# A rotary embedding on one core: the first reads all on one queue, x's first piece in three row groups ahead of the tables

## The chip, the cores and the metric

The kernel runs on one core of a Trainium2 chip. Its time is the device time of an execution in microseconds (us), and the figure for a kernel is the median of its runs. One more execution was recorded by the hardware profiler; all busy times, waits and transfers below are of that one.

## The reference

x has 8 images of 2048 positions, 8 heads and 64 numbers a head, all float32; the two tables, cos and sin, have 32 numbers for each position. The head's two halves are rotated against each other:

```python
x1 = x[..., : x.shape[-1] // 2]
x2 = x[..., x.shape[-1] // 2 :]
cos = cos[None, :, None, :]
sin = sin[None, :, None, :]
out1 = x1 * cos - x2 * sin
out2 = x1 * sin + x2 * cos
return np.concatenate([out1, out2], axis=-1)
```

Each image is 4.19 MB. All of x is read once and all of the output written once, 33.55 MB each way, and each table adds 0.26 MB.

## The kernel before

**Tiling.** The 2048 positions of an image are laid on 128 partitions, 16 positions to a partition, so that a partition ("row" below) holds 16 x 512 numbers, 32 KB, which lie in one run in memory. An image has one tile `xt` (five buffers, so that images 5 to 7 reuse those of 0 to 2), is computed in place, and is stored from the same tile. A unit (`UNIT`, L30) is a quarter of a row: 2048 numbers, 8 KB.

**Reads.** At the head of the program, the sines are read on the scalar queue (L74, into `sin_sb`), the cosines on the sync queue (L75, into `cos_sb`), and then `load` (L64 to L68) is called for images 0 to 4 on the sync queue. Image 0 is read in three pieces, of one, one and two units a row (1, 1 and 2 MB), all 128 rows each; the other images in one transfer of 4 MB. Images 5 to 7 are loaded as soon as image b - 5's arithmetic is written down in the program; the load itself waits until that image's stores have landed.

**Tables.** The scalar engine makes `nsin`, the sines with the other sign, and a copy of the sines in PSUM, `sin_ps` (L89, L90). The vector engine copies the cosines to PSUM, `cos_ps` (L92). GpSimd builds a unit matrix `eye` (L79, L80).

**Arithmetic.** `rotate` (L101) takes one piece of an image. In the usual kind, "A", GpSimd makes the sine products, one multiply for each half of the heads (L121, with `sin_sb` and then `nsin`); the vector engine makes the cosine products (L128) and adds the two into `xt` (L135). In kind "B", for the first unit of images 2, 4 and 5, the addition is done by the matrix engine with the unit matrix (L142, L143) and copied back by the scalar engine (L144). In kind "C", for the first unit of images 1 and 3, the vector engine makes the sine products too (L147), and the matrix engine adds (L159, L160, L164). Image 0 is computed in pieces of half a unit twice and then whole units, image 7 in whole units and at its end two halves.

**Stores.** `store` (L70 to L72) writes image 0 in three shares and images 1 to 6 in one, on the scalar queue; image 7 goes out in three shares (2, 1 and 1 MB) on the sync queue. A store is issued when the last addition of its share is done.

**Order.** `keep` holds the marked instructions of an engine in the order in which the program lists them. Each queue's transfers are issued in that order. The framework gives each transfer one of eight semaphores in turn, over both queues; a transfer that takes one over waits, before it is issued, for the transfer that had it before.

Of the kernel before, what the change touches and what calls it, by code (L numbers as in the profile page):

```python
# [10 lines left out]
def kernel(  # L11
# [7 lines left out]
    nc = tc.nc  # L19
    keep = tc.keep_in_program_order  # L20
# [5 lines left out]
    P = 128  # L26
# [8 lines left out]
    xv = x.rearrange("b (q r) h d -> b q (r h d)", q=P)  # L35
    ov = out.rearrange("b (q r) h d -> b q (r h d)", q=P)
    cos_src = cos.rearrange("(q r) d -> q r d", q=P)
    sin_src = sin.rearrange("(q r) d -> q r d", q=P)
# [9 lines left out]
    cos_sb = const_pool.tile([P, R, Dh], f32, tag="cb")  # L48
    sin_sb = const_pool.tile([P, R, Dh], f32, tag="sb")
# [8 lines left out]
    def spans(sizes):  # L58
        lo = 0
        for n in sizes:  # L60
            yield lo, n
            lo += n

    def load(b):  # L64
        xt = xpool.tile([P, ROW], f32, tag="xt", name=f"xt{b}")
        for lo, n in spans([UNIT, UNIT, 2 * UNIT] if b == 0 else [ROW]):
            keep(nc.sync.dma_start(out=xt[:, lo : lo + n], in_=xv[b, :, lo : lo + n]))  # L67
        xts[b] = xt  # L68

    def store(b, lo, n):  # L70
        queue = nc.sync if b == last else nc.scalar
        keep(queue.dma_start(out=ov[b, :, lo : lo + n], in_=xts[b][:, lo : lo + n]))  # L72

    keep(nc.scalar.dma_start(out=sin_sb, in_=sin_src))  # L74
    keep(nc.sync.dma_start(out=cos_sb, in_=cos_src))  # L75
    for b in range(NBUF):
        load(b)

# [2 lines left out]
        out=eye,  # L81
        in_=eye,
# [100 lines left out]
    for b in range(B):  # L183
        done = 0
        outs = list(spans(shares(b)))
        for lo, n in spans(pieces(b)):
            rotate(b, lo, n)
            done = lo + n
            while outs and sum(outs[0]) <= done:
                store(b, *outs.pop(0))  # L190
        if b + NBUF <= last:
            load(b + NBUF)
# [30 lines left out]
```

## Time and profile before

| | |
|---|---|
| median of 3 runs | 163.28 us (163.25 to 163.31) |
| the profiled execution, its own time | 163.36 us |
| its span, first to last instruction | 161.5 us |
| VectorE busy | 140.1 us (87%) |
| GpSimd busy | 138.9 us (86%) |
| TensorE matmuls busy | 49.8 us (31%) |
| ScalarE busy | 12.8 us (8%) |
| moved by DMA | 67.65 MB |
| GpSimd idle ahead of its first multiply, waiting for x | 6.0 us |

The span is shorter than the time of the execution by 1.86 us that lie around it. Busy times are of the five engines that compute; the transfers are done by 16 DMA engines beside them, which a queue of SyncE (q1 in the profile) and one of ScalarE (q10) feed. The page cuts the span into 40 slices of 4.04 us. "To landing" is the time from the issue of a transfer until its data is there, so it includes what the transfer stands in the queue. The chain of waits goes back from the last instruction: each step is what released the step after it.

At the head, the profile shows this in order of time: both tables are issued at 0.73 us, the cosines landing 3.7 and the sines 4.0 us later; x's first piece is issued at 1.15 us and lands after 6.0 us. VectorE's copy of the cosines runs at 4.46 us, its first multiply at 7.27, GpSimd's first multiply at 7.31, and the first addition at 9.81.

### The profile page before, as it was taken

What the parts mean: (1) busy time and instruction counts of PE and PEld (TensorE: products, weight loads), DVE (VectorE), ACT (ScalarE), POOL (GpSimd) and SP (SyncE); (2) the same over time, 40 slices, a digit from 0 to 9 for tenths busy, and PEclk for the clock granted to TensorE, in tenths of its full rate; (3) what the DMA queues carried; (4) which work ended last, traced back from release to release, by engine and by line L of the source; (5) the groups of instructions that cost most, each with busy time, mean ns of one, the idle gap of its engine ahead of it and who ended that gap; (6) DMA issues with size and microseconds to landing.
All of it is one profiled execution on the core that took longest, in us unless ns stands there. A gap on an engine that the chain in (4) does not pass through costs nothing.

```text
span 161.5 us, 460 instructions
## 1 busy us (share of the span) xinstructions
PE 49.8 (31%) x80; PEld 18.7 (12%) x80; DVE 140.1 (87%) x66; ACT 12.8 (8%) x14; POOL 138.9 (86%) x70
## 2 busy tenths in 40 slices
PE   0000000397507790788019741975000000000000
PEld 0000000132103230223014211421000000000000
DVE  0369899999999999999999999999899998999900
ACT  3300000002200201011200220022000000000000
POOL 1199999999999899999995999998999979999200
PEclk9999999999985899569955996599855555555555
DMA  4999999999999999999999998999999999999894
GB/s 147 432 448 418 438 438 454 406 406 503 389 389 446 422 495 389 422 487 389 422 487 389 438 473 381 438 471 398 446 448 406 438 454 406 438 454 434 377 422 211
DMA packets 3458, 67.65 MB, mean 419 GB/s; under 512 B 384, under 2 KB 384, under 8 KB 768
## 3 DMA queue, kind: packets, MB, share of 16 engines
q1 hardware_dynamic: 2016, 38.01, 55.3%
q10 hardware_dynamic: 1440, 29.62, 42.6%
q14 instruction: 2, 0.02, 0.0%
HBM read 34.08 MB, written 33.55 MB: 419 GB/s over the span
## 4 chain that ended last, share of the span: by engine, by line
DMA 46%; DVE 37%; POOL 9%; issue 2%; SPq 0%; DVEq 0%; POOLq 0%; ACTq 0%
DMA xt<-in_x_dram 28%; DVE t L128 18%; DMA out_dram<-xt 18%; DVE xt L135 17%; POOL t L121 9%; DVE t L147 1%; SPq L75 0%; DVEq L135 0%; POOLq L121 0%; SPq L67 0%; ACTq L72 0%
## 5 line engine op out<-in xcount | busy, mean ns | idle before, releaser
L121 POOL TENSOR_TENSOR t<-xt,sin_sb 128x1024 f32<-128x1024 f32 (+1 forms) x32 | 70.3, 2196 | 10.9 <-DMA xt<-in_x_dram 8.2
L128 DVE TENSOR_TENSOR t<-xt,cos_ps 128x2048 f32<-128x2048 f32 (+1 forms) x34 | 73.4, 2166 | 2.9 <-DMA xt<-in_x_dram 2.1
L121 POOL TENSOR_TENSOR t<-xt,nsin 128x1024 f32<-128x1024 f32 (+1 forms) x32 | 70.2, 2195 | 0.0
L135 DVE TENSOR_TENSOR xt<-t,t 128x2048 f32<-128x2048 f32 (+1 forms) x29 | 62.2, 2145 | 5.9 <-POOL t L121 3.4
L142 PE MATMUL o<-t,eye 128*128 128x512 f32 x24 | 17.3, 811 | 22.8 <-DVE t L128 19.3
L159 PE MATMUL o<-t,eye 128*128 128x512 f32 x16 | 12.1, 850 | 38.5 <-DVE t L128 36.3
L143 PE MATMUL o<-t,eye 128*128 128x512 f32 x24 | 14.9, 709 | 0.0
L144 ACT COPY xt<-o 128x1024 f32<-128x1024 f32 x6 | 6.1, 1012 | 45.7 <-PE o L143 45.7
L142 PEld LDWEIGHTS o<-t,eye 128*128 128x128 f32 x24 | 5.6, 256 | 32.2 <-issue 26.3
L159 PEld LDWEIGHTS o<-t,eye 128*128 128x128 f32 x16 | 3.7, 256 | 44.0 <-POOL t L121 30.9
L164 ACT COPY xt<-o 128x1024 f32<-128x1024 f32 x4 | 4.0, 1012 | 50.4 <-PE o L160 39.4
L143 PEld LDWEIGHTS o<-t,eye 128*128 128x128 f32 x24 | 5.7, 239 | 8.3 <-issue 8.3
L160 PE MATMUL o<-t,neye 128*128 128x512 f32 x8 | 6.4, 887 | 0.2 <-DVE t L147 0.2
L92 DVE COPY cos_ps<-cos_sb 128x512 f32<-128x512 f32 x1 | 0.7, 695 | 4.5 <-DMA cos_sb<-in_cos_dram 4.5
L147 DVE TENSOR_TENSOR t<-xt,sin_ps 128x2048 f32<-128x2048 f32 x2 | 4.6, 2280 | 0.0
L160 PE MATMUL o<-t,eye 128*128 128x512 f32 x8 | 4.1, 592 | 0.0
L160 PEld LDWEIGHTS o<-t,neye 128*128 128x128 f32 x8 | 2.2, 305 | 5.3 <-issue 3.7
L160 PEld LDWEIGHTS o<-t,eye 128*128 128x128 f32 x8 | 1.5, 190 | 1.9 <-issue 1.9
L89 ACT ACT_TABLE_LOAD x1 | 1.3, 1283 | 1.2 <-PEq L207 1.2
L89 ACT ACTIVATE nsin<-sin_sb 128x512 f32<-128x512 f32 x1 | 0.6, 630 | 2.3 <-DMA sin_sb<-in_sin_dram 2.3
L90 ACT COPY sin_ps<-sin_sb 128x512 f32<-128x512 f32 x1 | 0.6, 578 | 0.0
L79 POOL MEMSET eye<- 128x128 f32 x1 | 0.2, 204 | 0.3 <-POOLq L207 0.3
(6 smaller groups left out, 1.0 us busy)
## 6 DMA issues: line engine op xcount, KB each, us to landing
xt<-in_x_dram SPq DMA_DIRECT2D x7, 4096.0 KB, 39.1
out_dram<-xt ACTq DMA_DIRECT2D x6, 4096.0 KB, 28.0
xt<-in_x_dram SPq DMA_DIRECT2D x2, 1024.0 KB, 7.0
xt<-in_x_dram SPq DMA_DIRECT2D x1, 2048.0 KB, 12.5
out_dram<-xt ACTq DMA_DIRECT2D x1, 2048.0 KB, 25.1
out_dram<-xt SPq DMA_DIRECT2D x1, 2048.0 KB, 12.4
out_dram<-xt SPq DMA_DIRECT2D x2, 1024.0 KB, 8.7
out_dram<-xt ACTq DMA_DIRECT2D x1, 1536.0 KB, 19.9
```

Source lines behind the costliest of these rows:

```text
L89: keep(nc.scalar.mul(nsin, sin_sb, -1.0))
L92: keep(nc.vector.tensor_copy(cos_ps, cos_sb))
L121: nc.gpsimd.tensor_mul(out=t2u[:, :, u, :].rearrange("p (r h) d -> p r h d", h=H), in0=xu[:, :, 1 - u, :].rearrange("p (r h) d -> p r h d" ...
L128: nc.vector.tensor_mul(out=t1.rearrange("p (r k d) -> p r k d", r=nr, d=Dh), in0=xk, in1=rep(cos_ps[:, r0 : r0 + nr, :], 2 * H),)
L135: keep(nc.vector.tensor_add(out=xt, in0=t1, in1=t2))
L142: nc.tensor.matmul(oc, eye, t1[:, cs], start=True, stop=False)
L143: nc.tensor.matmul(oc, eye, t2[:, cs], start=False, stop=True)
L144: keep(nc.scalar.copy(xt[:, 2 * j * C : 2 * (j + 1) * C], o))
L147: nc.vector.tensor_mul(out=t2.rearrange("p (r k d) -> p r k d", r=nr, d=Dh), in0=xk, in1=rep(sin_ps[:, r0 : r0 + nr, :], 2 * H),)
L159: nc.tensor.matmul(oc, eye, t1u[:, gs, u, :], start=True, stop=False)
L160: nc.tensor.matmul(oc, eye if u else neye, t2u[:, gs, 1 - u, :], start=False, stop=True)
L164: nc.scalar.copy(xu[:, :, u, :], o.rearrange("p (g d) -> p g d", d=Dh))
```

## The change

All reads at the head are issued on the sync queue. `load` splits the first piece of image 0 (one unit a row) into three transfers by rows: rows 32 to 95, then 0 to 31, then 96 to 127. Right after them, from inside `load`, the sines and the cosines are read, and then image 0's other two pieces and the images 1 to 4 as before. The scalar queue reads nothing any more and only stores. The arithmetic, the pieces it is cut into, and the stores are the same. The lines of the file below `load` move down by up to nine and, behind the two removed lines, by seven.

```diff
     def load(b):
         xt = xpool.tile([P, ROW], f32, tag="xt", name=f"xt{b}")
         for lo, n in spans([UNIT, UNIT, 2 * UNIT] if b == 0 else [ROW]):
-            keep(nc.sync.dma_start(out=xt[:, lo : lo + n], in_=xv[b, :, lo : lo + n]))
+            first = b == 0 and lo == 0
+            for p, q in ((32, 96), (0, 32), (96, P)) if first else ((0, P),):
+                keep(
+                    nc.sync.dma_start(
+                        out=xt[p:q, lo : lo + n], in_=xv[b, p:q, lo : lo + n]
+                    )
+                )
+            if first:
+                keep(nc.sync.dma_start(out=sin_sb, in_=sin_src))
+                keep(nc.sync.dma_start(out=cos_sb, in_=cos_src))
         xts[b] = xt
 
     def store(b, lo, n):
         queue = nc.sync if b == last else nc.scalar
         keep(queue.dma_start(out=ov[b, :, lo : lo + n], in_=xts[b][:, lo : lo + n]))
 
-    keep(nc.scalar.dma_start(out=sin_sb, in_=sin_src))
-    keep(nc.sync.dma_start(out=cos_sb, in_=cos_src))
     for b in range(NBUF):
         load(b)
```

## The prediction

> **What bounds the kernel now.** I read the page's DMA rows first, then the busy times slice by slice, then the chain of waits, then the two ends of the span in time.
>
> ```profile
> GB/s 147 432 448 418 438 438 454 406 406 503 389 389 446 422 495 389 422 487 389 422 487 389 438 473 381 438 471 398 446 448 406 438 454 406 438 454 434 377 422 211
> DMA packets 3458, 67.65 MB, mean 419 GB/s; under 512 B 384, under 2 KB 384, under 8 KB 768
> q1 hardware_dynamic: 2016, 38.01, 55.3%
> q10 hardware_dynamic: 1440, 29.62, 42.6%
> ```
>
> The two queues hold the 16 DMA engines busy for 97.9% of 161.5 us. Per engine q1 (SyncE's, mostly reads) moves 38.01 MB / (0.553 x 16 x 161.5 us) = 26.6 GB/s, and q10 (ScalarE's, mostly writes) 29.62 / (0.426 x 16 x 161.5) = 26.9 GB/s: the same fixed rate per engine in both directions, some 430 GB/s together.
>
> The same in windows (last columns: share of the DMA engines' time, then GB/s):
>
> ```profile
> 1.00:1.50 0.50, 0.00 (x0) 0.00 (x0) 0.00 (x0) 0.33 (x1) 0.29 (x1) 1.00 0.00 0
> 1.50:2.00 0.50, 0.00 (x0) 0.00 (x0) 0.00 (x0) 0.50 (x1) 0.00 (x0) 1.00 0.67 66
> 2.00:2.50 0.50, 0.00 (x0) 0.00 (x0) 0.00 (x0) 0.45 (x1) 0.00 (x0) 1.00 0.18 20
> 2.50:3.00 0.50, 0.00 (x0) 0.00 (x0) 0.00 (x0) 0.00 (x0) 0.00 (x0) 1.00 0.83 213
> 3.00:3.50 0.50, 0.00 (x0) 0.00 (x0) 0.00 (x0) 0.00 (x0) 0.00 (x0) 1.00 0.99 385
> 3.50:4.00 0.50, 0.00 (x0) 0.00 (x0) 0.00 (x0) 0.00 (x0) 0.00 (x0) 1.00 1.23 479
> 4.00:40.00 36.00, 7.86 (x11) 2.92 (x12) 30.57 (x17) 2.36 (x4) 32.69 (x17) 1.00 1.02 434
> 40.00:130.00 90.00, 41.96 (x71) 15.80 (x69) 87.40 (x39) 9.11 (x9) 86.19 (x38) 0.77 1.00 432
> 130.00:159.00 29.00, 0.00 (x0) 0.00 (x0) 22.14 (x12) 0.00 (x0) 19.35 (x11) 0.50 0.99 427
> ```
>
> From 4 to 159 us the transfers never pause: 434, 432 and 427 GB/s. So the end is the start of the transfers plus 67.65 MB at that rate. Only the first 4 us are poor: they move (66 + 20 + 213 + 385 + 479) x 0.5 us = 0.58 MB, which at 432 GB/s is 1.35 us of work, so 2.65 us are lost before the stream is at speed.
>
> GpSimd and VectorE are nearly as full (86% and 87%), and the chain of waits runs through them, so I check whether they set the end instead:
>
> ```profile
> 63.33 29.16 DMA out_dram<-xt
> 92.56 39.12 DMA xt<-in_x_dram
> 131.81 4.61 POOL t L121 x2
> ```
>
> ```profile
> out_dram<-xt SPq DMA_DIRECT2D x1, 1024.0 KB, 7.3
> ```
>
> The second fence is the last store, issued at 153.40 (143.50 + 10.24 less its own 0.34 us). It moves 1.05 MB, 2.4 us at 432 GB/s, and with some 1.5 us for start and landing (the tables' first packets come about 1 us after their issue at 0.73) it would need 3.9 us; it takes 7.3. It stands about 3.4 us in a queue that is still full. The store of 29.16 us and the load of 39.12 us are likewise 4.19 MB each (9.7 us alone): queueing, not work. So an earlier or later computation changes nothing until it is more than about 3 us late at the end.
>
> **The change, part by part.** Bytes and packet sizes stay: the pieces of x keep 8 KB a row, the tables 2 KB a row. The two table reads move behind x's first piece and one of them changes queue; the first piece becomes three transfers.
>
> *(a) What the start-up slices hold.* In 1.5 to 2.5 us the engines moved 43 KB, 21 packets of 2 KB (the tables'), a little over one for each of the 16 engines; the packet records begin at 1.77 us. In that time packets came one by one, not at the rate of their bytes. Now 8 KB rows stand there. If the same 21 packets move, it is 172 KB instead of 43, and 129 KB at 432 GB/s are 0.30 us; an 8 KB packet, 8192 B / 26.6 GB/s = 0.31 us, fits between them. The slice 2.5 to 3.0 (213 GB/s) should fill up partly as well; half of its shortfall, 0.25 us, brings 0.12. I take 0.4 us of gain. Bounds: nothing, if the delay is of time and of bytes alike; 0.9 us, if the stream runs at full rate from 1.77 us on (4.00 - 1.77 - 1.35). A loss here I exclude: nothing is put ahead of the first transfer on SyncE, which still goes out at 0.73.
>
> *(b) Issuing.* SyncE issues seven transfers where it issued four, one each 0.47 us (starts 1.15, 1.63, 2.10). x's 64 rows are 0.52 MB, 1.2 us of transfer, the 32-row pieces 0.26 MB, 0.6 us each at full rate, the tables 0.6 us each: the list of work grows faster than it empties. Cost 0, hidden by the transfers ahead. If that cover were gone it would be two issues, 0.94 us, which I do not add to the range. In the compiled order x's image 1 now waits, before its issue, for the 64-row piece to land (images 2 to 4 for the sines, the cosines and x's last piece of image 0; before, images 2 to 4 waited for the sines and two x pieces). That is near 4 us, and x's two further pieces, 3.15 MB or 7.3 us, are queued by then; only SyncE's later loads stand behind it. Cost 0. ScalarE's queue loses one issue of 0.40 us ahead of a table load it has to do anyway; nobody waits for that.
>
> *(c) The 32-row pieces.* The trace has no transfer of fewer than 128 rows, so the price is bounded. At the rate of all rows, each 0.26 MB takes 0.61 us and the split is free: 0. That every engine keeps 26.6 to 26.9 GB/s on reads and writes alike says that a fixed path limits it, not the memory. If that path belongs to the engine, 32 rows go at full speed; if it belongs to the rows, 16 engines now crowd into a quarter of them. At half rate each piece takes 1.22 us, and both lose 2 x 0.61 = 1.22 us. The 64 rows could lose as much again, 1.22 us, if they too are too few; I take 0, because they move while the start-up leaves the engines waiting for time and not for bytes, and leave the upper end to the last tenth of the range. For the two pieces, between 0 and 1.22 the rows do not decide. I take 1.0 us: half rate, less some 0.2 us in which engines that share rows are out of step (the packet records show the engines ending the cosines up to 0.5 us apart, most within 0.2). The pieces stand one behind the other in each engine's list, which is why I let the second not run beside the first.
>
> [...]
>
> *(d) The computation's start.* GpSimd's first multiply (7.31 us) needs the whole first piece and the sines; VectorE's (7.27) the piece and the cosines. The bytes ahead of both are the same 1.57 MB. With (a) and (c) all three have landed at about 7.2 + 0.6 = 7.8 us; the sines 0.6 us before, near 7.2, so GpSimd starts about as before. The cosines come last: copy 0.69 us, then VectorE's multiply at 8.5 instead of 7.27. But the addition behind it waits for GpSimd's second multiply (9.81 now), so 8.5 + 1.23 = 9.7 still fits. Cost 0, covered by the 3.4 us at the end; without that cover up to 0.6 us.
>
> Sum: -0.4 + 0 + 1.0 + 0 = +0.6 us on the profiled execution's span of 161.5, so 162.1; with the 1.86 us that lie outside the span (163.36 - 161.5) 163.96, and less 0.08, by which that execution was above the median of 163.28, **163.9 us**. A measurement of this kernel tells about 0.2%, 0.33 us, from no change.
>
> **The rivals.** *Full rate for the 32 rows.* The path belongs to the engine, (c) costs nothing, (a) stays: 163.28 - 0.4 = 162.9, down to 162.4 with all of 0.9. For it: constant 26.6 and 26.9 GB/s per engine. Against: all rows of the trace give each engine its own eight rows, so they can't tell. It decides for faster when the two pieces together lose under 0.1 us. *Gain and loss cancel*, engines out of step by enough that (c) is 0.2 to 0.6, or the change of order does nothing and the pieces little: 163.3, within 0.3. For it: the spread of 0.5 us between engines. *The computation sets the end after all*: then GpSimd's start counts. At full rate the piece and the sines land one table (0.6 us) and the start-up gain (0.4) earlier, so the time is 163.28 - 1.0 = 162.3. Against: the last store's 3.4 us of queue. *Stores crowd out the last load*: an earlier first store takes turns with the loads sooner, image 7 lands later and its 21.6 us of arithmetic (131.81 to 153.38) end later; it decides from 3.4 us, the queue's slack, and a shift of 1 to 2 us in the load leaves it unused: 163.3, or 164.5 if the shift were 4.6 us.
>
> **How the numbers follow.** Forecast 58%, own range 163.5 to 164.5, the upper end being (c) whole and (a) nothing, 163.28 + 1.22 = 164.5; about 51 points of it lie above 163.61 and 7 within 0.2%. Full rate 27%: 18 points faster, 9 within. Cancelling 10%, all within. The computation 4%, faster. Stores 1%, slower. Together faster 0.22, same 0.26, slower 0.52. The range 162.7 to 164.5 leaves out the lower part of the full rate's bounds, the computation's case and a slow 64-row piece.
>
> **What would show it.** Right: the 8 KB packets of the first piece move more in 1.5 to 2.5 us than 43 KB; then a dip to about 215 GB/s for some 2 us between 3 and 6 us; from there 430 GB/s to the end, and the last store still queueing about 7 us. Each 32-row piece should land about 1.2 us after the one ahead. Wrong: landings 0.6 us apart and no dip (full rate), a start-up like before, (a) failing, or a pause in the transfers after 100 us, which would mean that the computation decides.

## The result, and the profile after

The changed kernel takes 164.71 us (median of 4 runs, 164.60 to 164.78), against 163.28 before on the same chip: slower by 1.43 us, a ratio of 1.0087 with a 95% interval of 1.0070 to 1.0105. The profiled execution took 164.78 us with a span of 163.0.

The windows of the changed kernel at the head (columns as above: the last two are the share of the DMA engines' time and GB/s):

```profile
1.50:2.00 0.50, 0.00 (x0) 0.00 (x0) 0.00 (x0) 0.50 (x1) 0.00 (x0) 1.00 0.00 0
2.00:2.50 0.50, 0.00 (x0) 0.00 (x0) 0.00 (x0) 0.01 (x1) 0.00 (x0) 1.00 0.85 147
2.50:3.00 0.50, 0.00 (x0) 0.00 (x0) 0.00 (x0) 0.00 (x0) 0.00 (x0) 1.00 0.82 197
3.00:4.00 1.00, 0.00 (x0) 0.00 (x0) 0.00 (x0) 0.00 (x0) 0.00 (x0) 1.00 0.84 336
4.00:5.00 1.00, 0.00 (x0) 0.00 (x0) 0.00 (x0) 0.00 (x0) 0.00 (x0) 1.00 1.17 320
5.00:6.00 1.00, 0.00 (x0) 0.00 (x0) 0.00 (x0) 0.00 (x0) 0.00 (x0) 1.00 0.91 217
6.00:7.00 1.00, 0.00 (x0) 0.00 (x0) 0.00 (x0) 0.00 (x0) 0.00 (x0) 1.00 0.95 219
7.00:8.00 1.00, 0.00 (x0) 0.00 (x0) 0.00 (x0) 0.00 (x0) 0.00 (x0) 1.00 1.09 399
```

From 5 to 7 us the engines are busy 91% and 95% of the time, and move 217 and 219 GB/s, half of the 430: they are not waiting, their packets take longer. From 5 to 6 us these are mostly the rows of x's 32-row pieces, from 6 to 7 us mostly those of the tables, which are queued behind them and have all 128 rows. And the first slice that moves anything is 2.0 to 2.5, where before it was 1.5 to 2.0. The records of the single packets say the same (8 KB packets are x's rows, 2 KB packets the tables'):

```
                              before      after
first packet of the stream    1.77 us     2.11 us
8 KB packet, median           309 ns      309 ns from 3.0 to 4.0 us, 519 to 577 ns from 4.5 to 6.0 us
2 KB packet, median           84 ns       139 to 152 ns from 5.5 to 7.0 us, then 85 to 89 ns
```

The loss can be added up in two windows, before and then after:

```profile
0.00:4.00 4.00, 0.00 (x0) 0.00 (x0) 0.00 (x0) 1.28 (x1) 0.70 (x6) 1.00 0.49 145
4.00:10.00 6.00, 0.00 (x0) 0.00 (x0) 2.12 (x3) 1.35 (x3) 2.69 (x3) 1.00 1.03 438
```

```profile
0.00:4.00 4.00, 0.00 (x0) 0.00 (x0) 0.00 (x0) 1.28 (x1) 0.70 (x6) 1.00 0.42 127
4.00:10.00 6.00, 0.00 (x0) 0.00 (x0) 0.56 (x1) 1.22 (x3) 1.07 (x1) 1.00 1.03 335
```

In the first 4 us the changed kernel moves (145 - 127) x 4 us = 0.07 MB less, 0.17 us at 432 GB/s; in the next 6 us (438 - 335) x 6 us = 0.62 MB less, 1.43 us. Together 1.6 us, and the span grew by 1.5. (A window counts a packet whole where it starts; with packets that cross an edge shared out, the second figure is 1.3 us.)

The chain of waits of the changed kernel tells another story. Its shares by line:

```profile
by line: DVE t L135 35.3%; DVE xt L142 29.9%; POOL t L128 17.1%; issue 5.8%; DMA sin_sb<-in_sin_dram 3.9%; DVE t L154 1.3%; SPq L70 1.0%; DVEq L142 0.3%; POOLq L128 0.0%
```

The long transfers that stood in it before are gone; it is now arithmetic from the sines to the end, and GpSimd's first multiply begins at 8.93 us instead of 7.31, 1.62 us later, about what the kernel lost. So two readings give the same number, and the time alone can't choose between them: the stream of transfers lost 1.5 us, or the computation began 1.6 us late.

### The profile page after: what moved, and what is told of

Read it like the earlier page. It is cut to its first block, busy times and chain, and to the rows that moved or that the text cites. A ratio compares the mean times of both kernels' runs of the same rounds, so it can differ in the third digit from the quotient of the medians.

```text
span 163.0 us, 464 instructions
## 1 busy us (share of the span) xinstructions
PE 49.0 (30%) x80; PEld 18.4 (11%) x80; DVE 140.1 (86%) x66; ACT 12.8 (8%) x14; POOL 139.1 (85%) x70
## 4 chain that ended last, share of the span: by engine, by line
DVE 66%; POOL 17%; issue 6%; DMA 4%; SPq 1%; DVEq 0%; POOLq 0%
DVE t L135 35%; DVE xt L142 30%; POOL t L128 17%; DMA sin_sb<-in_sin_dram 4%; DVE t L154 1%; SPq L70 1%; DVEq L142 0%; POOLq L128 0%
## 5 line engine op out<-in xcount | busy, mean ns | idle before, releaser
L166 PE MATMUL o<-t,eye 128*128 128x512 f32 x16 | 12.0, 842 | 40.2 <-POOL t L128 32.5
L149 PE MATMUL o<-t,eye 128*128 128x512 f32 x24 | 16.7, 787 | 23.5 <-DVE t L135 20.1
L150 PE MATMUL o<-t,eye 128*128 128x512 f32 x24 | 14.9, 709 | 0.0
L167 PE MATMUL o<-t,eye 128*128 128x512 f32 x8 | 4.1, 592 | 0.0
```

Of the source, the lines that this page charges most:

```text
L149: nc.tensor.matmul(oc, eye, t1[:, cs], start=True, stop=False)
L150: nc.tensor.matmul(oc, eye, t2[:, cs], start=False, stop=True)
L166: nc.tensor.matmul(oc, eye, t1u[:, gs, u, :], start=True, stop=False)
L167: nc.tensor.matmul(oc, eye if u else neye, t2u[:, gs, 1 - u, :], start=False, stop=True)
```

## The experiments

All figures are medians with the ratio to the kernel before on the same chip. "Stream" below is the two-window sum above, worked out for each kernel from its one profiled execution: the bytes by which it falls short of the kernel before from 0 to 4 and from 4 to 10 us, divided by 432 GB/s.

**Which of the two sets the end.** The kernel before, with GpSimd made late by work that nothing needs:

```diff
+    waste = const_pool.tile([P, 4, Dh], f32, tag="waste")
+    for _ in range(12):
+        keep(nc.gpsimd.tensor_mul(out=waste, in0=nsin[:, :4, :], in1=sin_sb[:, :4, :]))
```

> The kernel before with twelve multiplies of 128x128 on GpSimd that nothing needs, ahead of its first multiply, so that it begins some 1 to 2 us later; all transfers as before. Theory (transfers set the end): 163.3 us, the last store queues that much less than 7.3 us. Rival (the computation sets it): the time grows by what GpSimd's first multiply is later than 7.31, to 164.3 to 165.3 us.

163.48 us, ratio 1.0014 (1.0005 to 1.0022). GpSimd came even later than meant; its timeline in this run:

```profile
10.87 0.45 POOL L96 TENSOR_TENSOR waste<-nsin,sin_sb 128x128 f32<-128x128 f32 x1
11.28 1.25 POOL L125 TENSOR_TENSOR t<-xt,sin_sb 128x512 f32<-128x512 f32 x1
```

The first multiply began 3.97 us later, and the time grew by 0.16. The last store shows where the rest went:

```profile
out_dram<-xt SPq DMA_DIRECT2D x1, 1024.0 KB, 4.0
```

It was issued 3.44 us later than before, at 156.84 us, and lands 4.0 us after its issue, where before it took 7.3: the 3.3 us are the queue that it no longer stood in, and 4.0 is close to the 3.9 us that such a store was reckoned to need by itself. The computation has some 3.4 us to spare at the end. In the changed kernel the last store, issued at 154.92 us, still takes 7.1, so it is not the computation that lost the time, whatever the chain of waits runs through.

**Split or order.** The changed order with the first piece in one transfer (against the kernel before, with the lines between left out):

```diff
             keep(nc.sync.dma_start(out=xt[:, lo : lo + n], in_=xv[b, :, lo : lo + n]))
+            if b == 0 and lo == 0:
+                keep(nc.sync.dma_start(out=sin_sb, in_=sin_src))
+                keep(nc.sync.dma_start(out=cos_sb, in_=cos_src))
 ...
-    keep(nc.scalar.dma_start(out=sin_sb, in_=sin_src))
-    keep(nc.sync.dma_start(out=cos_sb, in_=cos_src))
```

> The changed order without the split: x's first piece as one transfer of all 128 rows, then sines and cosines, all on the sync queue. Theory (the stream of transfers sets the end; the 32-row pieces move at half rate, some 1.3 us, and the start-up got some 0.2 us worse): 163.5 us, packets of 8 KB at 309 ns throughout. Rival (the computation sets the end, and it began 1.6 us later in the changed kernel, at 8.93 instead of 7.31): here GpSimd should begin near 6.8 to 7.0, so 162.8 to 163.0 us. If the order and not the split is what cost, 164.7 us.

163.46 us, ratio 1.0008 (1.0000 to 1.0017). GpSimd's first multiply began at 6.20 us, 1.1 us earlier than before, and no time was gained by it. And the split with the tables first, on two queues as before:

```diff
-            keep(nc.sync.dma_start(out=xt[:, lo : lo + n], in_=xv[b, :, lo : lo + n]))
+            for p, q in ((32, 96), (0, 32), (96, P)) if b == 0 and lo == 0 else ((0, P),):
+                keep(nc.sync.dma_start(out=xt[p:q, lo : lo + n], in_=xv[b, p:q, lo : lo + n]))
```

> The split without the changed order: both tables first on their two queues as before, then 64, 32 and 32 rows. Theory: 163.28 + 1.3 = 164.6 us, a dip to about 200 to 250 GB/s of some 2.4 us, and a start-up like before. If the split is free and the order cost: 163.3 us. The computation as the bound gives 164.6 us too, since the piece lands 1.3 us later, so this run tells the split from the order and nothing more.

164.24 us, ratio 1.0054 (1.0042 to 1.0066), 0.92 us slower than before. Its windows show the dip where the pieces now stand:

```profile
4.00:5.00 1.00, 0.00 (x0) 0.00 (x0) 0.69 (x1) 0.65 (x2) 0.00 (x0) 1.00 1.06 442
5.00:6.00 1.00, 0.00 (x0) 0.00 (x0) 0.00 (x0) 0.70 (x2) 0.00 (x0) 1.00 1.18 320
6.00:7.00 1.00, 0.00 (x0) 0.00 (x0) 0.00 (x0) 0.00 (x0) 0.00 (x0) 1.00 1.08 254
7.00:8.00 1.00, 0.00 (x0) 0.00 (x0) 0.00 (x0) 0.00 (x0) 0.00 (x0) 1.00 0.78 279
```

The split costs by itself, the order next to nothing. But 0.92 and 0.14 do not make 1.43: split and order together cost some 0.4 us more than each alone. The packet records name two places for it: behind the pieces the tables ran at 139 to 152 ns a packet (84 in the run with the split alone, where they stand ahead), and the stream began at 2.11 us (1.75 in that run). What the tables' packets took over 84 ns, added up from 4 to 10 us and shared among the 16 engines, is 0.46 us; in the run with the order alone it is 0.09.

**Is it the rows.** The same order and sizes, cut along the row so that every transfer has all 128 rows:

```diff
-            first = b == 0 and lo == 0
-            for p, q in ((32, 96), (0, 32), (96, P)) if first else ((0, P),):
+            cuts = (0, n // 2, 3 * n // 4, n) if b == 0 and lo == 0 else (0, n)
+            for c0, c1 in zip(cuts, cuts[1:]):
                 keep(
                     nc.sync.dma_start(
-                        out=xt[p:q, lo : lo + n], in_=xv[b, p:q, lo : lo + n]
+                        out=xt[:, lo + c0 : lo + c1], in_=xv[b, :, lo + c0 : lo + c1]
```

> The changed kernel with the first piece cut in three transfers of the same sizes (0.52, 0.26, 0.26 MB) along the row and not by rows, so that each has all 128 rows (4, 2 and 2 KB a row). Theory: the rows and not the number of transfers cost, so no dip, 163.5 us, a little more for packets of 2 KB (150 against 309 ns for four times the bytes would show it). If three transfers in place of one cost by themselves: 164.7 us.

164.04 us (163.67 to 164.34), ratio 1.0044 (1.0031 to 1.0057): a miss. Packets kept their speed (medians of 159 ns for 4 KB, 84 for 2 KB), as the theory said, but this cut costs 0.7 us in another way. The window shows it:

```profile
5.00:6.00 1.00, 0.00 (x0) 0.00 (x0) 0.00 (x0) 0.00 (x0) 0.00 (x0) 1.00 0.91 277
```

Four transfers of 2 KB rows now stand one behind the other on one queue, and several engines stand idle between two packets (only 11 to 12 of the 16 are busy from 5.0 to 5.4 us), where the 32-row pieces kept them busy (in the changed kernel 16 or more packets are under way at any moment from 4.5 to 7.0 us); single packets of 2 KB took up to 642 ns. So the run doesn't settle what it was made for; the next one does.

**Which rows.** The first piece as two halves, rows 0 to 63 and 64 to 127:

```diff
-            for p, q in ((32, 96), (0, 32), (96, P)) if first else ((0, P),):
+            for p, q in ((0, 64), (64, P)) if first else ((0, P),):
```

> The changed kernel with the first piece cut in rows 0 to 63 and rows 64 to 127 in place of 64, 32 and 32. [...] If it is the number of rows that counts, 64 rows being nearly enough (as rows 32 to 95 were, at 309 ns): 163.5 to 164.2 us. A first issue of 0.58 us again would show that fewer rows than 128 make the first transfer start late; 0.37 us that it was something else.

165.45 us, ratio 1.0126 (1.0113 to 1.0139), 2.1 us slower than before:

```profile
4.00:5.00 1.00, 0.00 (x0) 0.00 (x0) 0.00 (x0) 0.00 (x0) 0.00 (x0) 1.00 0.98 221
5.00:6.00 1.00, 0.00 (x0) 0.00 (x0) 0.00 (x0) 0.00 (x0) 0.00 (x0) 1.00 1.06 238
6.00:7.00 1.00, 0.00 (x0) 0.00 (x0) 0.00 (x0) 0.00 (x0) 0.00 (x0) 1.00 0.83 170
7.00:8.00 1.00, 0.00 (x0) 0.00 (x0) 0.00 (x0) 0.00 (x0) 0.00 (x0) 1.00 1.01 248
```

64 rows, rows 0 to 63, move at half rate, and so do rows 64 to 127 behind them: 540 to 621 ns for an 8 KB packet from 3.5 to 7.0 us (medians of half a microsecond each). The slices from 6 us on hold the tables too. 64 rows, rows 32 to 95, moved at 309 ns in the changed kernel. So it is not the number of rows but which: in these two runs rows of one half of the partitions got about half the rate (519 to 621 ns a packet), rows spread over both halves the whole (309). From 4 to 6 us, where x's rows alone move, this run shows 221 and 238 GB/s.

**Two at a time.** Rows 96 to 127 on the scalar queue, so that they are in flight beside the others:

```diff
+                queue = nc.scalar if p == 96 else nc.sync
                 keep(
-                    nc.sync.dma_start(
+                    queue.dma_start(
```

> The changed kernel with rows 96 to 127 read on the scalar queue, so that they are in flight beside rows 32 to 95 and 0 to 31. Theory: if two transfers to different rows share the engines well, the half rate is hidden and the loss goes from about 1.4 to 0.2 to 0.5 us, 163.5 to 163.8; if the engines do them in step, row against row, it stays at 164.3 to 164.7 us.

164.12 us (163.86 to 164.53), ratio 1.0045 (1.0032 to 1.0059): 0.6 us better than the changed kernel, short of the hoped-for 0.9 or more. Its stream begins at 1.77 us, with the scalar queue's rows, so most of the 0.6 may be the start and not the sharing; the next two runs, on one queue, lose as little.

**The late start.** The order of the three groups, changed so that 32 rows come first:

```diff
-            for p, q in ((32, 96), (0, 32), (96, P)) if first else ((0, P),):
+            for p, q in ((96, P), (0, 32), (32, 96)) if first else ((0, P),):
```

> The changed kernel with its three row groups in the order 96 to 127, 0 to 31, 32 to 95. The stream of transfers starts with its first packet at 2.11 us in the changed kernel, 2.07 with rows 0 to 63 first, 1.74 to 1.77 with all 128 rows, with a table, or with rows 96 to 127 on the scalar queue. If it is the 64 rows that start late: first packet near 1.77 and 164.3 to 164.6 us. If any group of fewer rows on the sync queue starts late: near 2.1 and 164.7 us.

```diff
-            for p, q in ((32, 96), (0, 32), (96, P)) if first else ((0, P),):
+            for p, q in ((0, 32), (32, 96), (96, P)) if first else ((0, P),):
```

> The same in the order 0 to 31, 32 to 95, 96 to 127. If it is the 64 rows that start late: first packet near 1.77. If it is the row at which a group begins (0 or 32 late, 96 not): near 2.1 us here and 1.77 with rows 96 to 127 first. The time stays at 164.3 to 164.8 us in either case, since both quarters move at half rate.

First packets at 1.78 and 1.75 us, first issues of 0.39 us (0.58 in the changed kernel); 164.15 us, ratio 1.0044 (1.0015 to 1.0073), and 164.16 us, ratio 1.0056 (1.0034 to 1.0078). A group of 64 rows started late as the first transfer of all, whether it begins at row 32 (2.11 us) or at row 0 (2.07), and a group of 32 rows (1.75 and 1.78) or of 128 (1.74 to 1.77) did not. Against the kernel before, these orders lose 0.82 and 0.83 us where the changed kernel loses 1.43, the intervals just overlapping. Not all of the 0.6 need be the 0.34 us of the late start: with 32 rows first, one of the two half-rate groups also moves while the start-up leaves engines idle anyway (with rows 96 to 127 first, a busy share of 0.81 from 1.5 to 2.0 us and 0.55 from 2.0 to 2.5). Why 64 rows start late no run tells.

The two runs also show what slows the tables. Behind rows 32 to 95 they ran at a median of 84 ns a packet from 5.5 us on, with 0.15 us in sum over that; behind rows 96 to 127 at 159 ns from 5.5 to 6.0 us, with 0.42 us. In all four runs in which a half-rate group stands directly ahead of the tables that sum is 0.41 to 0.50 us, and behind the whole piece it is 0.09. Why a half-rate group slows a transfer of all rows behind it, no run tells.

**Other places for the tables.** x's first piece whole and first on the sync queue, both tables on the scalar queue:

```diff
-    keep(nc.sync.dma_start(out=cos_sb, in_=cos_src))
+    keep(nc.scalar.dma_start(out=cos_sb, in_=cos_src))
```

> The kernel before with both tables on the scalar queue and x's first piece, whole, first on the sync queue. Theory: the start-up is that of the run with the order alone (0.4 us more moved by 4 us than before) and nothing is at half rate: 163.0 to 163.4 us, at best 0.2 us faster than before. If the queue that starts with the tables holds up the other: 163.5 us or more.

163.43 us, ratio 1.0012 (0.9999 to 1.0025): no gain. And the kernel before with nothing but the sines moved to the sync queue, tried twice:

```diff
-    keep(nc.scalar.dma_start(out=sin_sb, in_=sin_src))
+    keep(nc.sync.dma_start(out=sin_sb, in_=sin_src))
```

> The kernel before with the sines moved to the sync queue and nothing else: both tables still ahead of x. Theory (the queue by itself is worth nothing): 163.3 us. If a second queue helps the start-up, one queue should move less in the first 4 us and take 163.5 us or more.

> The kernel before with the sines on the sync queue, once more, since its executions lay between 163.35 and 172.92 us. If that spread belongs to the kernel, it comes again; if it came from elsewhere: 163.3 to 163.6 us throughout.

The executions lay between 163.35 and 172.92 us the first time (median 168.4; three of twelve at 163.35 to 163.95, no different from before) and between 165.85 and 170.2 the second (median 169.37 of four), with the granted clock at 0.756 to 0.775 in short and long ones alike. The spread came again on another chip, while the kernel before beside it had a median of 163.33 (163.25 to 164.35), so it belongs to this kernel. The window behind the tables, in a long execution (170.98 us) of the first of the two, the kernel before first:

```profile
3.50:5.50 2.00, 0.00 (x0) 0.00 (x0) 0.69 (x1) 0.79 (x2) 0.00 (x0) 1.00 1.09 452
```

```profile
3.50:5.50 2.00, 0.00 (x0) 0.00 (x0) 0.69 (x1) 1.35 (x3) 0.00 (x0) 1.00 0.81 335
```

The packet records do not name the engine, but the starts can be laid to the ends: in the kernel before, from 3 to 10 us, a packet starts 4 ns (median) after another's end. So read, four engines end their part of the tables between 3.50 and 3.62 us and start on x's rows between 5.53 and 5.91, some 2 us later, while the other twelve go on; the second time, in an execution of 170.2 us, one engine stood still for about 1.5 us. As many engines are late at the end. Of the last image's load twelve parts are done at 129.3 to 130.5 us and four at 138.8 to 138.9, the second time fifteen by 130.4 and one at 138.1; in the kernel before all sixteen are done between 130.2 and 131.2. GpSimd waits 17.2 us for x in the first of the two in place of 8.2. In the run with the order alone, with the same two tables behind x's piece on one queue, no engine pauses for more than 0.15 us between 3 and 9 us, and the executions lie between 163.34 and 163.62. Why the engines stand still is open, and so is how 2 us at the head become 8 to 10 at the end.

| kernel | stream, 0 to 4 us | stream, 4 to 10 us | sum, us | time against before, us |
|---|---|---|---|---|
| the changed kernel | 127 GB/s | 335 GB/s | +1.6 | +1.43 |
| halves | 115 | 287 | +2.4 | +2.11 |
| 32 rows first, 96 to 127 | 150 | 374 | +0.8 | +0.82 |
| 32 rows first, 0 to 31 | 152 | 374 | +0.8 | +0.83 |
| split alone | 166 | 370 | +0.75 | +0.92 |
| one group on the scalar queue | 162 | 378 | +0.7 | +0.78 |
| cut along the row | 174 | 395 | +0.3 | +0.72 |
| order alone | 190 | 438 | -0.4 | +0.14 |
| tables on the scalar queue | 165 | 442 | -0.2 | +0.09 |
| late computation | 176 | 448 | -0.4 | +0.16 |

Losses of the stream are found in the time to within 0.4 us. (The largest difference, in the run cut along the row, is that its profiled execution, 163.67 us, was its shortest.) Gains are not: the three streams that start 0.2 to 0.4 us better end no sooner. Added up packet by packet, they have lost their lead by 60 us, and the changed kernel, 1.5 us behind at 10 us, is 1.2 behind from 50 us on. No version beat the kernel before.

## Why the prediction was wrong

**What bounds the kernel** was right: 4 us of lateness in the computation cost 0.16 us, and the reckoned slack of 3.4 us was the 3.3 that the last store gave up.

**Step (c), the 32-row pieces, was right on the half rate, and failed in what it left out.** That rate was the author's estimate: no transfer of the kernel before has fewer than 128 rows, so no run on record then showed the term of 1.0 us; what the runs showed in its place is 519 to 577 ns for an 8 KB packet of these rows against 309. The pieces move at half rate, 217 GB/s from 5 to 6 us, in the dip that was forecast (from 3 to 6 us; it lay between 5 and 7, and its second half was the tables'). They landed some 1.4 and 0.7 us after the piece ahead, where 1.2 was named for each. Their price was about right: what x's packets took over 309 ns from 4 to 10 us, shared among 16 engines, is 0.83 us in the changed kernel and 1.04 in the run with the split alone, against the 1.0 that was taken and 1.22 as the bound. But the step priced the pieces and put at nothing, without a reason, what stands in the queue behind them. The tables' packets at 139 to 152 ns took another 0.46 us. So the term measured 1.43 from 4 to 10 us by the windows (1.3 with the packets shared out), over its bound; with the tables first it measured 0.94.

**Step (a), the start-up, failed**, as the prediction put it: a gain of 0.4 us with a loss excluded, "nothing is put ahead of the first transfer". It measured a loss of 0.17 us by 4 us. With the whole piece first the gain is there in full ((190 - 145) x 4 us = 0.18 MB, 0.42 us at 432 GB/s; from 1.5 to 2.5 us 19 packets of 8 KB began, where the step counted on 21); but the first transfer was one of 64 rows, and that one took 0.58 us to issue and began 0.34 us late, so that 9 packets began in that time. What was excluded is what happened. The sign that was named for this step, more than 43 KB from 1.5 to 2.5 us, came true all the same (147 GB/s for 0.5 us is 74 KB): it was too weak, because it did not ask for what had moved by 4 us. And even where the start-up gained, the kernel did not: the run with the order alone loses it again later, as the rates from 22 to 28 us show, the kernel before first, then that run:

```profile
22.00:28.00 6.00, 0.00 (x0) 0.00 (x0) 5.86 (x3) 0.00 (x0) 6.00 (x3) 1.00 0.91 377
```

```profile
22.00:28.00 6.00, 0.00 (x0) 0.00 (x0) 5.86 (x4) 0.00 (x0) 4.16 (x3) 1.00 0.88 336
```

(377 - 336) x 6 us is 0.25 MB, 0.57 us. Of the 32 KB packets there, 34 of 49 took 1.3 to 1.7 us (17 of 53 in the kernel before), where 1.21 is the median elsewhere; the cause was not found.

**Step (b), issuing**, put at nothing, holds for the changed kernel's list, but not as a rule: 2 KB rows, transfer behind transfer on one queue, left engines idle in the run cut along the row (11 to 12 of 16 busy from 5.0 to 5.4 us) and with the sines moved (a busy share of 0.81 from 3.5 to 5.5 us).

**Step (d)** had GpSimd beginning about as before, near 7.2 us; it began at 8.93. That cost nothing, by the slack named for it.

With -0.4 replaced by +0.17 and 1.0 by 1.43 the sum is 1.6 for a measured 1.43. The forecast of 163.9 had the direction and the half rate; the time lies 0.2 us over the end of its range, which had been set by a loss-free start-up and a bound that held only for the pieces themselves. The rivals fell: the full rate to the half-rate packets, the cancelling to the sum, the computation to the run with GpSimd late, the crowded-out last load to the 7.1 us of the last store, slack of the queue that it would have had to use up.

## What to carry to other kernels

Where the transfers never pause, count the bytes that the stream misses, window by window, and read the busy share beside them: here 0.91 and 0.95 at 217 and 219 GB/s were slow packets (519 to 577 ns in place of 309 for x's rows, 139 to 152 in place of 84 for the tables'), and 0.81 at 335 GB/s, with the sines moved, was engines that stood still. Then look at which transfer's packets are slow: here a third of the slow time was the tables', queued behind the pieces. Of the transfers into part of the partitions, rows 32 to 95, spread over both halves, kept 309 ns a packet; rows of one half alone took 519 to 621 ns, and the tables' packets queued behind them 139 to 160 ns in place of 84. A chain of waits that runs through arithmetic from end to end does not show that the arithmetic sets the time: look how long the last store stands in its queue, or make the arithmetic late and see.

## What the runs showed that was not expected

A first transfer of 64 rows started 0.3 us later than one of 32 or 128 (first packet at 2.07 and 2.11 us against 1.74 to 1.78). A single issue moved from one queue to the other made the kernel before unsteady: with both tables ahead of x on the sync queue one or four engines stood idle for 1.5 to 2.4 us in the two profiled executions, as many engines ended the last load 8 to 10 us behind the others, and executions took up to 9.6 us more (172.92 against 163.34). And the tables, transfers of all 128 rows, ran slower directly behind one into a single half of the partitions: 2 KB packets at 139 to 160 ns in place of 84.
